# Earlier value-block loads, earlier first-pair steps, a split of the input scales, and FFN weight sums on VectorE in a hybrid attention, convolution and FFN block

## The chip, the cores and the metric

One NeuronCore of a Trainium2 chip runs the whole block. TensorE (PE) multiplies, with its weight loads shown as PEld; VectorE (DVE), ScalarE (ACT) and GpSimd (POOL) do the elementwise work; SyncE (SP) issues most of the DMAs, in the order of its own queue. The metric is device time in microseconds, the median of several runs. A profile is one execution with its trace.

## The reference

A decoder block over 1024 tokens of width 1024, everything in float32:

```python
h = rms_norm(x, g_pre_mix)
z = h @ w_in                     # q, k, v (3 groups x 8 heads x 64), conv input 2 x 1024, two gates 1024
y_attn = dilated_attention_mixer(q, k, v, rel_bias_table, w_attn_out)
y_conv = conformer_conv_mixer(glu_in, b_glu, w_dw, b_dw, g_ln, b_ln, w_conv_out, b_conv_out)
x = x + rms_norm((sigmoid(z_ga) * y_attn + sigmoid(z_gc) * y_conv) @ w_mix_out, g_post_mix)
h = rms_norm(x, g_pre_ffn)
gate, up = split(h @ w_ffn_in)   # 2 x 2816
x = x + rms_norm((silu(gate) * up) @ w_ffn_out, g_post_ffn)
```

The attention has three groups of eight heads (windows of 128, 512 and 2048 tokens with dilations 1, 4 and 16); the convolution is causal, depthwise, 31 wide, with a sigmoid gate before it and a layer norm and silu behind it.

## The kernel before

**Precision.** Each float32 operand is split into a high part and a low part of a short type, and a product is three matmuls (high by high, high by low, low by high). Weights are split into float16 parts with a scale that is a power of two, found from the weight itself: `peaks` (L122) squares the block on ACT (L129) with the row sums as a by-product, `total` rounds them (L135 or L137) and multiplies them with a matrix of ones on PE (L144), and `scales` turns the result into the scale on DVE (L145, L147, L155, L156). `scaled_parts` (L282) then makes the parts: ACT writes the high part (L283), DVE the low part (L284). The input's two scales, for the first half of the block (C_PRE) and for the FFN (C_PREF), are made the same way from the two gain vectors in `input_scales` (L165).

**Winograd pairs.** Most weights are handled as pairs of blocks, one Winograd step of 2 by 2 with seven products instead of eight (`winograd`, L455). Its products run into a few PSUM banks one after the other, X, Z and V: ACT copies X and V out at L464, L469 and L474, and the functions f11, f12, f21, f22 add the results on DVE. f22 (L1912 in the FFN, L987 for queries and keys) reads bank X, and the last product (A22 by T4) is added into X only after that. The sums of the weights' quarters are made in `quarters` (L296): step c = 1 makes two sums (L312, L313), c = 3 two more (L319, L320), and the steps c = 0, 2, 4, 5 split a block each. All four sums are issued on the engine `self.wsplit`, which is GpSimd while the convolution runs beside the pairs and again from L1697 on (that is, in the mixing product and the FFN). The right-hand side's sums are made in `quarter_sums` (L492): a first loop (L507, L508) and a second one (L516 on `wsplit`, L517 on DVE); each sum is split by ACT (L1339) and DVE (L1340).

**Order.** The order is written out by hand. Each engine runs its instructions in the order in which the program issues them, and the program issues matmuls and, between them, other steps. A `tick()` follows every third matmul of 512 columns (or every sixth of 256 columns in the value stage); `later(n, step)` puts a step n ticks after now, and generators given to `bg` are advanced by one step a tick. `ready(jobs, load, peaks, scales, parts)` (L374) plans the preparation of weight blocks: at which tick they are loaded, squared, scaled and split. `pair(i)` (L401) does this for the next Winograd pair while the present one is multiplied; `timed(now, then)` (L393) does it for the value blocks. `load_ahead(i)` issues the DMA loads (L259) of all blocks up to i that are not on their way yet, on SP's queue, each into a buffer: a slot "b" (42 of them), or, for the first block of a pair, one of three ring buffers "d". 

**Stages** (us in the profiled execution):

- *Start* (to 47): the first blocks against the raw input. `input_scales` is finished after the last matmul of the start; behind it stand the first gate's DVE additions (L735).
- *Gates, conv input* (to 160): single blocks, then the first two Winograd pairs. Their preparation is planned in `build` by one `ready` call and two `later` calls. In the same part of SP's queue stand the bias lines of the attention (L596) and their write to 1024 rows (L599).
- *Pairs of conv input, gates, queries and keys* (to 551), with the depthwise convolution on DVE, ACT and PE beside them.
- *Values* (551 to 710): six value blocks of 256 columns (`v`, L1069), matmuls L1090, L1092 and L1094 into two PSUM banks, evicted by ACT at L1100 and L1102 and stored at L1077. Beside them run the convolution's layer norm (`conv_norm`: statistics L531, DVE L1373 and L1379, ACT L1376, silu L1395, stores L1397) and the attention, which reads back queries and keys (L1015, L1016, L1022), the bias lines (L609) and values (L1052). L1188 are its first products.
- *Rest of the attention, output and mixing products* (to 1085).
- *FFN input* (1085 to 1493): PLAIN single blocks (L1796 silu, L1798 product), then twenty Winograd pairs (f11 L1907, f22 L1912, f12 L1916), and sums of the results for the output product (`sums`, L1773 to L1790), stored on SP; `plain_sums` does the latter for the single blocks.
- *FFN output* (to the end): L2021.

Of the kernel before, what the change touches and what calls it, by code (L numbers as in the profile page):

```python
# [20 lines left out]
KT = 8  # L21
# [44 lines left out]
def f(ap):  # L66
    return ap if ap.dtype == F16 else ap.bitcast(F32)


class Build:  # L70
# [94 lines left out]
    def input_scales(self):  # L165

        nc = self.nc
        self.gain, self.unscale, self.top = [], [], []
        p = []
        for c in (C_PRE, C_PREF):  # L170
            m = self.tiny(2, "pk", 4)
            nc.scalar.activation(self.junk[:, :8], self.col8(c), AF.Square, scale=1 / H_TOP, accum_out=m[:, 0:1])
            p.append(self.total(m, 1))
        yield 6
        for e, c in enumerate((C_PRE, C_PREF)):
            t = self.small.tile([128, 5], F32, name=f"hs{e}")
            self.bound(t[:, 0:1], p[e])
            nc.vector.reciprocal(t[:, 1:2], t[:, 0:1])
            for k, x in enumerate((1.0, -1.0, 0.125)):
                nc.vector.tensor_scalar(t[:, 2 + k:3 + k], t[:, 0:1], x, None, op0=OP.mult)  # L180
            g = self.small.tile([128, 8], F32, name=f"hg{e}")
            nc.vector.tensor_scalar(g, self.col8(c), t[:, 1:2], None, op0=OP.mult)
            self.gain.append(g)
            self.unscale.append(t[:, 2:5])
            self.top.append(t[:, 1:2])
            yield 1

    stag = "s"

# [200 lines left out]
        for k, x in zip(parts, todo, strict=True):  # L390
            self.later(k, x)

    def timed(self, now, then):  # L393

        self.load_ahead(now[-1])
        self.queue_split(now[-1])
        self.flush(now[-1])
        self.ready(then, 1, 8, 20, (22, 24, 27, 30)[:2 * len(then)])
        return [self.hl.pop(i) for i in now]

    def pair(self, i):  # L401


        J = self.jobs
        self.load_ahead(i)
        self.queue_split(i)
        self.flush(i)
        n, t = i + 1, self.ticks
        todo = [(1, lambda: self.quarters(i, 3)), (8, lambda: self.quarters(i, 4)), (10, lambda: self.quarters(i, 5))]
        if n < len(J) and J[n][2] == "row1":  # L410
            if n + 2 < len(J) and J[n + 2][2] == "row1":
                todo += [(LF, lambda: self.load_ahead(n + 3)), (PK, lambda: self.peaks(n + 3))]
            if n + 1 in self.pre:
                todo += [(PRE + c, lambda c=c: self.prescale(n + 1, c)) for c in range(2)]
            todo += [(SC, lambda: self.scales(n + 1))]
            todo += [(k, lambda c=c: self.quarters(n + 1, c)) for c, k in enumerate(PC)]
            if self.conv_sums:
                todo.append((22, self.channel_sum))
            self.queued = n + 2
        elif n < len(J):  # L420
            self.ready((n, n + 1), 2, 9, 18, (20, 22, 24, 26))
        for k, s in todo:
            self.plan.setdefault(t + k, []).append(s)
        return self.hl[i]
# [189 lines left out]
    def start(self, jobs):  # L614


        nc = self.nc
        n = len(jobs)
# [64 lines left out]
        for kt in range(KT):  # L683
            s = slice(kt * 128, (kt + 1) * 128)
            for i in range(n):
                for a, b in ((W[i][0], self.hH), (W[i][0], self.hL), (W[i][1], self.hH)):
                    for hf in range(2):
                        nc.tensor.matmul(banks[i][hf], a[:, s], b[kt][:, hf * H:(hf + 1) * H],  # L688
                                         start=kt == 0 and a is W[i][0] and b is self.hH,
                                         stop=kt == KT - 1 and a is W[i][1])  # L690
                self.tick()
            if kt == KT - 1:
                for _ in ns:
                    pass
            if kt == KT - 3:
                next(norm)
            if kt == KT - 2:
                try:
                    next(norm)
                except StopIteration as e:  # L700
                    pb = e.value
        self.rs = self.slot()
        for hf in range(2):
            nc.scalar.copy(self.rs[:, hf * H:(hf + 1) * H], pb[hf])
        self.xs = xs
        return banks

    def renorm(self):
# [357 lines left out]
        self.nc.gpsimd.tensor_tensor(d[:, :, 1], y, f(d[:, :, 0]), op=OP.subtract)  # L1066
        return v

    def v(self, g, hg, now, then):  # L1069

        nc = self.nc
        W = self.timed(now, then)
        un = self.scale[now[0]][1]

        def out(i, x):
# [416 lines left out]
def build(ctx, tc, aps):  # L1492
# [81 lines left out]
    conv = B.conv()  # L1574
    next(conv)
    i = glu_pairs[0]
    B.ready((i - 1, i), 10, 22, 30, (32, 33, 36, 38, 42))
    B.later(34, lambda: B.load_ahead(i + 2))
    B.later(44, lambda: B.peaks(i + 2))
    for j in range(3, FIRST):  # L1580
        u_out(j, B.glu(j, glu_jobs[j][1], B.gate(j, glu_jobs[j][0])))

# [51 lines left out]
    att = B.attention()  # L1634
    vs = list(vj.values()) + [late[:1] or co[:1]]
    for i, (g, hg) in enumerate(vj):
        B.v(g, hg, vs[i], vs[i + 1])
        if i == 0:
            next(att)
            B.fine = att  # L1640
# [152 lines left out]
    def ffn_half(j, hf, W):  # L1793
# [4 lines left out]
        nc.vector.scalar_tensor_tensor(o, ps, B.scale[fi[j][1]][1], o, op0=OP.mult, op1=OP.mult)  # L1798
        held[j, hf] = o

    Ws, i = [], fi[PLAIN][1]
    B.ready((i - 1, i), 1, 16, 28, (42, 44, 50))
    B.later(46, lambda: B.load_ahead(i + 2))
    B.later(58, lambda: B.peaks(i + 2))
    for j in range(PLAIN):
# [13 lines left out]
    for j in range(0, PLAIN, 2):  # L1819
# [8 lines left out]
                q.clear()  # L1828

        for n in range(3):  # L1830
            B.later(6 + 5 * n + j, lambda n=n, f=plain_sums: f(n))


    NP = FT // 2
# [302 lines left out]
```

## Time and profile before

| | |
|---|---|
| time, median of 3 runs | 1709.87 us (1708.0 to 1711.88) |
| the profiled execution | 1711.49 us |
| its span, mean granted clock | 1709.6 us, 0.991 |
| PE busy | 1654.3 us (97%), 8757 matmuls |
| DVE busy | 1272.2 us (74%) |
| ACT busy | 992.7 us (58%) |
| POOL busy | 599.0 us (35%), 468 instructions |

A row of the timeline gives the start, the length, the engine, the line, what it writes and reads, the shape, how many instructions of one kind the row holds, and in brackets the idle time in front of it with what ended it. SPq is a DMA in SP's queue, from the issue of the first to that of the last in the row. Windows give the same by stretches: busy time and count of each engine, the granted TensorE clock (1.00 is full), the share of the DMA engines and the bandwidth. A busy PE is not PE at its peak: at a clock of 0.50 it is busy as well.

### The profile page before, as it was taken

The page shows a single profiled execution, that of the slowest core. Times are in us where ns is not written, and L with a number is a line of the kernel's source. Part 1 is how long each engine was busy: PE and PEld are TensorE (multiplying, and loading weights), DVE is VectorE, ACT ScalarE, POOL GpSimd, SP SyncE. Part 2 cuts the span into 40 slices and gives each one's busy share as a digit, 9 for nine tenths or more (in the row PEclk, how much of TensorE's full clock was granted, in tenths as well). Part 3 has the DMA queues.
Part 4 walks back from the last instruction along what each step waited for, and adds up shares of the span by engine and source line. Part 5 has one row for each costly group of instructions (what it writes and reads, how often), then busy time and mean ns, then how long its engine had stood idle before and what let it go on. Part 6 is the DMA issues. An engine that isn't in the chain of part 4 may idle for free.

```text
span 1709.6 us, 25078 instructions
## 1 busy us (share of the span) xinstructions
PE 1654.3 (97%) x8757; PEld 1064.7 (62%) x8757; DVE 1272.2 (74%) x2383; ACT 992.7 (58%) x1875; POOL 599.0 (35%) x468
## 2 busy tenths in 40 slices
PE   8989999999999899989999999989999999999998
PEld 7634444444444789989888878534444444488886
DVE  6879999999999566698764756586666665677686
ACT  6475667766665587768622357654545545454463
POOL 0005777787785145646400120133342333100000
PEclk9999999999999999999999999999999999999999
DMA  4352334355656879887934732223233232394244
GB/s 166 114 188 97 105 140 150 135 186 180 202 161 170 255 237 252 220 229 217 314 142 184 276 127 87 80 76 116 93 123 118 92 130 93 128 376 136 98 137 154
DMA packets 159481, 277.06 MB, mean 162 GB/s; under 512 B 46993, under 2 KB 78412, under 8 KB 159356
## 3 DMA queue, kind: packets, MB, share of 16 engines
q1 hardware_dynamic: 155148, 263.30, 46.6%
q0 software_dynamic: 3920, 11.91, 2.2%
q8 instruction: 69, 1.13, 0.3%
q14 instruction: 56, 0.46, 0.1%
q10 hardware_dynamic: 288, 0.27, 0.0%
HBM read 184.81 MB, written 95.33 MB: 164 GB/s over the span
## 4 chain that ended last, share of the span: by engine, by line
PE 75%; DVE 10%; DMA 4%; ACT 4%; POOL 3%; issue 3%; SPq 1%; DVEq 0%; ACTq 0%; POOLq 0%
PE p L2021 12%; PE p L450 11%; PE p L452 11%; PE p L451 11%; PE p L1747 4%; PE p L434 4%; PE p L438 4%; PE p L436 4%; DVE p L829 3%; PE p L688 2%; PE p L1188 2%; PE p L1090 2%; PE p L1092 2%; PE p L1094 2%; PE p L1224 2%
## 5 line engine op out<-in xcount | busy, mean ns | idle before, releaser
L450 PE MATMUL p<-b,b 128*128 128x512 f16 x1032 | 393.1, 381 | 5.6 <-ACT c L464 5.0
L452 PE MATMUL p<-b,b 128*128 128x512 f16 x1032 | 393.3, 381 | 2.8 <-POOL b L293 2.8
L451 PE MATMUL p<-b,b 128*128 128x512 f16 x1032 | 393.2, 381 | 0.0
L2021 PE MATMUL p<-b,b 128*128 128x512 f32 x924 | 209.8, 390 | 0.0
L2021 PEld LDWEIGHTS p<-b,b 128*128 128x128 f32 x924 | 173.5, 188 | 36.1
L452 PEld LDWEIGHTS <-b 128*128 128x128 f16 x1032 | 101.0, 98 | 128.6 <-POOL b L293 6.5
L450 PEld LDWEIGHTS <-b 128*128 128x128 f16 x1032 | 101.2, 98 | 126.4 <-issue 6.3
L451 PEld LDWEIGHTS <-b 128*128 128x128 f16 x1032 | 101.0, 98 | 124.2 <-issue 8.5
L312 POOL TENSOR_TENSOR d<-b 128x512 f32<-128x512 f32 x42 | 60.5, 1440 | 306.0 <-DVE b L284 217.3
L829 DVE SCALAR_TENSOR_TENSOR p<-b,par,p 128x511 f32<-128x511 f32 (+14 forms) x232 | 163.9, 739 | 0.0
L434 PE MATMUL p<-b,b 128*128 128x512 f32 (+1 forms) x368 | 146.1, 397 | 4.7 <-ACT b L283 2.4
L438 PE MATMUL p<-b,b 128*128 128x512 f32 (+1 forms) x368 | 145.2, 394 | 0.1
L436 PE MATMUL p<-b,b 128*128 128x512 f32 (+1 forms) x368 | 145.1, 394 | 0.0
L293 POOL TENSOR_TENSOR b<-d,b 128x1024 f16<-128x1024 f32 x44 | 96.1, 2184 | 81.7 <-ACT b L292 81.5
L1090 PE MATMUL p<-b,b 128*128 128x256 f16 x384 | 107.1, 279 | 9.9 <-ACT d L1100 9.9
L284 DVE SCALAR_TENSOR_TENSOR b<-d,sc,b 128x1024 f16<-128x1024 f32 x40 | 53.1, 1328 | 75.1 <-ACT b L283 75.1
L1092 PE MATMUL p<-b,b 128*128 128x256 f16 x384 | 107.2, 279 | 0.0
L1094 PE MATMUL p<-b,b 128*128 128x256 f16 x384 | 107.1, 279 | 0.0
L1340 DVE TENSOR_TENSOR b<-b,b 128x512 fp32r<-128x512 f32 (+1 forms) x117 | 85.3, 731 | 22.7 <-ACT b L1339 21.3
L1339 ACT CAST b<-b 128x512 fp32r<-128x512 f32 (+1 forms) x117 | 72.0, 618 | 43.0 <-PE p L2021 18.0
L1340 DVE TENSOR_TENSOR b<-c,b 128x512 fp32r<-128x512 f32 (+1 forms) x101 | 70.3, 696 | 33.5 <-ACT b L1339 33.3
L1201 ACT ACTIVATE c<-c,stat 128x128 f32<-128x128 f32 (+1 forms) x192 | 84.8, 445 | 12.2 <-DVE stat L1191 12.0
(273 smaller groups left out, 3697.3 us busy)
## 6 DMA issues: line engine op xcount, KB each, us to landing
b<-w_in SPq DMA_DIRECT2D x30, 512.0 KB, 7.4
dk<-c SPq DMA_DIRECT2D x48, 256.0 KB, 2.6
dq<-c SPq DMA_DIRECT2D x48, 256.0 KB, 3.4
b<-dq SPq DMA_DIRECT2D x48, 256.0 KB, 8.7
b<-dk SPq DMA_DIRECT2D x48, 256.0 KB, 9.9
b<-w_fi SPq DMA_DIRECT2D x24, 512.0 KB, 4.9
d<-w_in SPq DMA_DIRECT2D x23, 512.0 KB, 4.8
dqS<-c SPq DMA_DIRECT2D x44, 256.0 KB, 2.0
```

The lines of the kernel that those rows point to most:

```text
L434: nc.tensor.matmul(ps, hi[:, s], a, start=kt == 0, stop=False)
L436: nc.tensor.matmul(ps, hi[:, s], b, start=False, stop=False)
L438: nc.tensor.matmul(ps, lo[:, s], a, start=False, stop=kt == nk - 1)
L450: nc.tensor.matmul(ps, hi[:, s], a, start=first and kt == 0, stop=False, skip_group_check=True)
L451: nc.tensor.matmul(ps, hi[:, s], b, start=False, stop=False, skip_group_check=True)
L452: nc.tensor.matmul(ps, lo[:, s], a, start=False, stop=kt == 3, skip_group_check=True)
L829: nc.vector.scalar_tensor_tensor(A[i][:, j:], src[i][:, :H - j], w[i], A[i][:, j:], op0=OP.mult, op1=OP.add)
L1090: nc.tensor.matmul(o, a, hi[:, s], start=kt == 0, stop=False)
L1092: nc.tensor.matmul(o, a, lo[:, s], start=False, stop=False)
L1094: nc.tensor.matmul(o, b, hi[:, s], start=False, stop=kt == KT - 1)
L1340: nc.vector.tensor_tensor(s[:, 512:512 + n], src, f(s[:, :n]), op=OP.subtract)
L2021: nc.tensor.matmul(acc[t], x, y, start=first and e == 0, stop=last and e == 2, skip_group_check=True)
```

## The change

Five edits, all in the order of steps or the engine of one operation; the arithmetic is the same.

1. `input_scales` yields between its two sets. `start` calls for the first one a step of kt earlier (KT-2), and the second one runs as a background generator after the start.
2. `timed` no longer loads the next value block at tick 1. It loads two blocks ahead at tick 14, and the steps for the next block are at 17 and 19 to 25 where they were at 20 and 22 to 30. The last pair of queries and keys loads the second value block at its tick 16.
3. The first Winograd pairs: load at tick 2 (was 10), squares at 14 (22), scale at 24 (30), parts from 26 (32); the second pair's load at 22 (34) and squares at 37 (44).
4. `wsplit` is set to VectorE before the FFN. So 84 GpSimd additions of 128x512 (L312, L313, L319, L320 of twenty pairs, and four of L516) go to DVE.
5. The FFN's first pair: squares at tick 12 (16), scale at 22 (28), parts at 24, 26, 30 (42, 44, 50); `plain_sums` 24 ticks later.

```diff
--- before.py
+++ after.py
@@ -173,6 +173,8 @@
             p.append(self.total(m, 1))
         yield 6
         for e, c in enumerate((C_PRE, C_PREF)):
+            if e:
+                yield 12
             t = self.small.tile([128, 5], F32, name=f"hs{e}")
             self.bound(t[:, 0:1], p[e])
             nc.vector.reciprocal(t[:, 1:2], t[:, 0:1])
@@ -183,7 +185,6 @@
             self.gain.append(g)
             self.unscale.append(t[:, 2:5])
             self.top.append(t[:, 1:2])
-            yield 1
 
     stag = "s"
 
@@ -390,12 +391,14 @@
         for k, x in zip(parts, todo, strict=True):
             self.later(k, x)
 
-    def timed(self, now, then):
+    def timed(self, now, then, after):
 
         self.load_ahead(now[-1])
         self.queue_split(now[-1])
         self.flush(now[-1])
-        self.ready(then, 1, 8, 20, (22, 24, 27, 30)[:2 * len(then)])
+        self.ready(then, None, 8, 17, (19, 21, 23, 25)[:2 * len(then)])
+        if after:
+            self.later(14, lambda: self.load_ahead(after[-1]))
         return [self.hl.pop(i) for i in now]
 
     def pair(self, i):
@@ -419,6 +422,7 @@
             self.queued = n + 2
         elif n < len(J):
             self.ready((n, n + 1), 2, 9, 18, (20, 22, 24, 26))
+            self.later(16, lambda: self.load_ahead(n + 3))
         for k, s in todo:
             self.plan.setdefault(t + k, []).append(s)
         return self.hl[i]
@@ -689,11 +693,10 @@
                                          start=kt == 0 and a is W[i][0] and b is self.hH,
                                          stop=kt == KT - 1 and a is W[i][1])
                 self.tick()
-            if kt == KT - 1:
-                for _ in ns:
-                    pass
             if kt == KT - 3:
                 next(norm)
+            if kt == KT - 2:
+                next(ns)
             if kt == KT - 2:
                 try:
                     next(norm)
@@ -703,6 +706,7 @@
         for hf in range(2):
             nc.scalar.copy(self.rs[:, hf * H:(hf + 1) * H], pb[hf])
         self.xs = xs
+        self.bg(ns)
         return banks
 
     def renorm(self):
@@ -1066,10 +1070,10 @@
         self.nc.gpsimd.tensor_tensor(d[:, :, 1], y, f(d[:, :, 0]), op=OP.subtract)
         return v
 
-    def v(self, g, hg, now, then):
-
-        nc = self.nc
-        W = self.timed(now, then)
+    def v(self, g, hg, now, then, after):
+
+        nc = self.nc
+        W = self.timed(now, then, after)
         un = self.scale[now[0]][1]
 
         def out(i, x):
@@ -1574,9 +1578,9 @@
     conv = B.conv()
     next(conv)
     i = glu_pairs[0]
-    B.ready((i - 1, i), 10, 22, 30, (32, 33, 36, 38, 42))
-    B.later(34, lambda: B.load_ahead(i + 2))
-    B.later(44, lambda: B.peaks(i + 2))
+    B.ready((i - 1, i), 2, 14, 24, (26, 27, 31, 34, 40))
+    B.later(22, lambda: B.load_ahead(i + 2))
+    B.later(37, lambda: B.peaks(i + 2))
     for j in range(3, FIRST):
         u_out(j, B.glu(j, glu_jobs[j][1], B.gate(j, glu_jobs[j][0])))
 
@@ -1634,7 +1638,7 @@
     att = B.attention()
     vs = list(vj.values()) + [late[:1] or co[:1]]
     for i, (g, hg) in enumerate(vj):
-        B.v(g, hg, vs[i], vs[i + 1])
+        B.v(g, hg, vs[i], vs[i + 1], vs[i + 2] if i < 5 else None)
         if i == 0:
             next(att)
             B.fine = att
@@ -1798,8 +1802,9 @@
         nc.vector.scalar_tensor_tensor(o, ps, B.scale[fi[j][1]][1], o, op0=OP.mult, op1=OP.mult)
         held[j, hf] = o
 
+    B.wsplit = nc.vector
     Ws, i = [], fi[PLAIN][1]
-    B.ready((i - 1, i), 1, 16, 28, (42, 44, 50))
+    B.ready((i - 1, i), 1, 12, 22, (24, 26, 30))
     B.later(46, lambda: B.load_ahead(i + 2))
     B.later(58, lambda: B.peaks(i + 2))
     for j in range(PLAIN):
@@ -1828,7 +1833,7 @@
                 q.clear()
 
         for n in range(3):
-            B.later(6 + 5 * n + j, lambda n=n, f=plain_sums: f(n))
+            B.later(30 + 5 * n + j, lambda n=n, f=plain_sums: f(n))
 
 
     NP = FT // 2
```

In the changed program the lines stand up to five further down: L259 is L260, L312 and L313 are L313 and L314, L964 is L968, L1912 is L1917.

SP's queue around the first read-back of queries and keys (w_v are the value weights, two DMAs a block, here the third block; dconv the convolution's blocks, dq and dk queries and keys, rep the bias lines). Before:

```order
L1356 DMA b_5201<-dconv_70 128x1024
L1356 DMA b_5230<-dconv_71 128x1024
L1356 DMA b_5263<-dconv_72 128x1024
L1015 DMA b_5381<-dq_98 64x1024
L1016 DMA b_5382<-dq_98 64x1024
L1015 DMA b_5385<-dq_98 64x1024
L1016 DMA b_5386<-dq_98 64x1024
L1022 DMA b_5389<-dk_97 64x1024 x2
L1022 DMA b_5392<-dk_97 64x1024 x2
L609 DMA c_5395<-rep_699 128x2x256
L259 DMA b_5404<-w_v 128x1024
L259 DMA b_5406<-w_v 128x1024
```

After:

```order
L1360 DMA b_5201<-dconv_70 128x1024
L260 DMA b_5224<-w_v 128x1024
L260 DMA b_5226<-w_v 128x1024
L1360 DMA b_5234<-dconv_71 128x1024
L1360 DMA b_5277<-dconv_72 128x1024
L1019 DMA b_5385<-dq_98 64x1024
L1020 DMA b_5386<-dq_98 64x1024
L1019 DMA b_5389<-dq_98 64x1024
```

The third value block's load has moved from behind the read-backs to between two loads of the convolution. The second block's, further up in the same queue, has moved ahead of four stores of queries and keys and one store of the convolution; the fourth block's from behind the first two silu stores (L1397) to right behind the next value read-back (L1052), and the fifth's to behind the silu stores, ahead of the next read-back of queries and keys.

DVE in one of the twenty FFN pairs, from the second split of the pair's late quarters to f12 (c_13073 to c_13075 are the pair's result halves, p the banks, d_13165 the next pair's two sums). Before:

```order
L1907 TENSOR_TENSOR c_13073<-p_13072,c_13073 128x512
L284 SCALAR_TENSOR_TENSOR c_13121<-b_12860,sc_12942,c_13121 128x512
L284 SCALAR_TENSOR_TENSOR b_13156<-d_12996,sc_13085,b_13156 128x1024
L1912 TENSOR_TENSOR c_13075<-p_13071,c_13075 128x512
L1916 TENSOR_TENSOR c_13074<-p_13131,c_13074 128x512
L284 SCALAR_TENSOR_TENSOR b_13193<-d_13165,sc_13085,b_13193 128x1024
```

After:

```order
L1912 TENSOR_TENSOR c_13073<-p_13072,c_13073 128x512
L285 SCALAR_TENSOR_TENSOR c_13121<-b_12860,sc_12942,c_13121 128x512
L285 SCALAR_TENSOR_TENSOR b_13156<-d_12996,sc_13085,b_13156 128x1024
L313 TENSOR_TENSOR d_13165<-b_12998 128x512
L314 TENSOR_TENSOR d_13165<-d_13165,d_12996 128x512
L1917 TENSOR_TENSOR c_13075<-p_13071,c_13075 128x512
L1921 TENSOR_TENSOR c_13074<-p_13131,c_13074 128x512
L285 SCALAR_TENSOR_TENSOR b_13193<-d_13165,sc_13085,b_13193 128x1024
```

The two sums stand between the split of the next pair's first block and f22; before, they were on POOL.

ACT at the first Winograd pair (b_787 and b_883 are single blocks, d_ and b_ behind L129 the pair's two weight blocks, pb their rounded row sums). Before:

```order
L283 ACTIVATE b_957<-b_787,sc_935 128x512
L1339 CAST b_966<-b_249 128x512
L737 ACTIVATE b_885<-p_931,par,sc_820 128x512
L129 ACTIVATE junk,pk_990<-b_883 128x1024
L137 CAST pb_992<-pk_990 128x1
L1339 CAST b_1000<-c_997 128x512
L1339 CAST b_1000<-b_250 128x512
L129 ACTIVATE junk,pk_1016<-d_947 128x1024
L129 ACTIVATE junk,pk_1016<-b_949 128x1024
L135 ACTIVATE pb_1019<-pk_1016 128x1
```

After:

```order
L129 ACTIVATE junk,pk_972<-d_899 128x1024
L129 ACTIVATE junk,pk_972<-b_901 128x1024
L135 ACTIVATE pb_975<-pk_972 128x1
L284 ACTIVATE b_957<-b_787,sc_939 128x512
L1343 CAST b_966<-b_249 128x512
L741 ACTIVATE b_885<-p_935,par,sc_820 128x512
L129 ACTIVATE junk,pk_995<-b_883 128x1024
L137 CAST pb_997<-pk_995 128x1
L1343 CAST b_1005<-c_1002 128x512
L1343 CAST b_1005<-b_250 128x512
```

The pair's squares have moved from behind the single block's square to seven places further up.

## The prediction

> **What bounds the kernel now.** I read the page's busy shares and the chain that ended last, then what the matmul engine (PE) waited for, then windows around each wait, then the timeline there.
>
> ```profile
> span 1709.6 us, 25078 instructions
> PE 75%; DVE 10%; DMA 4%; ACT 4%; POOL 3%; issue 3%; SPq 1%; DVEq 0%; ACTq 0%; POOLq 0%
> ```
>
> The last chain runs three quarters of the span through PE, so time is won only where PE stands still or runs at a reduced clock. The list of PE's waits (total, times, longest) says where:
>
> ```profile
> PE p L1090 <- ACT d L1100: 9.9, 2, 6.3
> PE p L450 <- ACT c L464: 5.0, 1, 5.0
> PE p L144 <- ACT pb L135: 4.5, 3, 2.7
> PE p L450 <- DVE c L987: 3.1, 4, 1.2
> PE p L434 <- ACT b L283: 2.4, 1, 2.4
> PE p L434 <- DVE b L735: 2.3, 1, 2.3
> PE p L1473 <- ACT b L1479: 1.9, 2, 1.1
> ```
>
> All but the L987 line belong to places that the change touches: the start (2.3), the first two Winograd pairs (2.4 and, of L144's three, 0.45 and 2.7), the value stage (9.9), the front of the FFN (5.0, L144's third of 1.4, and 0.8 of L1473's). The granted clock adds to them. Windows (length, then busy time and count of PE, its weight loads, DVE, ACT, POOL, then clock, DMA share, GB/s):
>
> ```profile
> 47.50:50.00 2.50, 2.50 (x12) 2.05 (x11) 2.29 (x4) 0.52 (x1) 0.00 (x0) 1.00 0.00 0
> 107.50:110.00 2.50, 2.50 (x7) 0.83 (x8) 2.43 (x8) 1.17 (x3) 0.00 (x0) 0.50 0.00 0
> 125.00:127.50 2.50, 2.50 (x7) 0.89 (x6) 0.00 (x0) 2.50 (x4) 0.00 (x0) 0.50 0.88 320
> 590.00:595.00 5.00, 3.96 (x20) 2.83 (x19) 0.00 (x0) 2.82 (x5) 1.49 (x2) 0.50 0.33 96
> 595.00:600.00 5.00, 5.00 (x49) 4.64 (x48) 2.63 (x5) 1.29 (x3) 2.28 (x2) 0.99 0.04 12
> 620.00:625.00 5.00, 4.70 (x23) 3.96 (x23) 1.25 (x8) 4.97 (x8) 1.49 (x2) 0.50 0.86 326
> 1130.00:1135.00 5.00, 2.05 (x5) 0.69 (x5) 4.93 (x12) 3.50 (x7) 0.00 (x0) 0.60 0.01 2
> 1135.00:1140.00 5.00, 5.00 (x18) 2.01 (x17) 4.93 (x8) 1.80 (x3) 0.00 (x0) 0.71 0.31 116
> ```
>
> After most of these stalls the clock is 0.50: 7 matmuls of 512 columns in 2.5 us instead of 12, so such a window loses about 1.1. In the value stage 20 matmuls took 3.96 where 49 take 5.00, a loss of 1.9; after its second stall 23 took 4.70, a loss of 2.3. The FFN's two windows lose 0.97 and 1.1. A stall therefore costs its length and 1 to 2 us more.
>
> **The change, part by part.** Sums are made against the profiled execution: 1711.49 us, which is the span and 1.9 around it. The median of the runs is 1709.87, 1.6 lower.
>
> *Input scale.* Before, DVE works out two sets behind the start's last matmul:
>
> ```profile
> 44.45 0.16 DVE L145 TENSOR_SCALAR hs<-p 128x1 int32<-128x1 int32 x1 [7.81 <-PE p L144]
> 45.97 1.28 DVE L735 TENSOR_TENSOR b<-p,b 128x512 f32<-128x512 f32 x2
> ```
>
> L735 makes the gate that the next matmul waits for. Both sets stand in front of it (44.45 to 45.97). Now the first is done a step of the start earlier, inside the 7.81 in which DVE was idle, and the second comes a few ticks later on an idle DVE. L735 needs only its bank and the norm, both there before the last matmul. The 2.3 goes: **2.25**, with no loss of clock to win (47.5 to 50 stands at 1.00).
>
> *First pairs.* The loads of the first pair pass the 1024-row write of the bias line in SP's queue, those of the second pass a line write, a store and the next such write; squares, scale and parts move up with them.
>
> ```profile
> 99.94 1.06 ACT L129 ACTIVATE junk<-d 128x1024 bf16<-128x1024 f32 x1 [2.42 <-DMA d<-w_in]
> 102.75 0.16 PE L144 MATMUL p<-pb,ones 128*128 128x1 bf16 x1 [0.45 <-ACT pb L135]
> 123.02 0.16 PE L144 MATMUL p<-pb,ones 128*128 128x1 bf16 x1 [2.71 <-ACT pb L135]
> ```
>
> ACT waited 2.42 for the weights, and everything behind was late: 0.45 here, the 2.4 of L434 next, 1.1 of clock; at the second pair 2.71 and 1.1. Together 7.8. What is late next: the pair's two squares (1.06 each, some 2.4 with what belongs to them) now stand ahead of the early block's square on ACT, and PE comes to the two blocks' L144s one behind the other. If ACT's former idle time of 2.42 takes them in, nothing is lost; if they simply push the early block's square back, PE stands up to 2.4. I take 1.8, nearer to the upper end, since that idle time now lies behind the squares and only casts stand between. **6.0** is left (5 to 7.8).
>
> *Value stage.* Before, a value block is loaded when the one ahead of it starts:
>
> ```profile
> 563.44 3.02 SPq L1356 DMA_DIRECT2D b<-dconv  x4
> 577.52 1.41 SPq L259 DMA_DIRECT2D b<-w_v  x2
> 587.57 1.06 ACT L129 ACTIVATE junk<-b 128x1024 bf16<-128x1024 f32 x1 [7.67 <-DMA b<-w_v]
> 609.25 1.29 SPq L259 DMA_DIRECT2D b<-w_v  x2
> 617.02 1.06 ACT L129 ACTIVATE junk<-b 128x1024 bf16<-128x1024 f32 x1 [1.36 <-DMA b<-w_v]
> 625.79 3.44 SPq L1022 DMA_DIRECT2D b<-dk  x4
> ```
>
> The third block's load is issued at 577.52, behind the stacked queries and keys, and lands 10 us later. ACT stands 7.67 in front of its square, and the eviction L1100, queued behind the square, frees PE's bank 6.3 too late. Now that load stands among the convolution's loads of 563.44, 11 to 14 us earlier, so it lands by about 576 and the square does not wait. 6.3 and 1.9 of clock go: 8.2. At 609.25 the same happens with the fourth block (stall 9.9 - 6.3 = 3.6, clock 2.3); its load now stands right behind the value load of 584.80, ahead of eight stores. 14.1 in all. The loads need free slots: if one waits, the key stores and convolution loads queued behind it on SP wait too.
>
> What is late next here: ACT's waits of 1.47 and 1.36 go, which brings the second eviction 2.8 of the 3.6 forward, so up to 0.8 stays; the first exponentials follow ACT's chain, about 1.1; the second stack's key loads (625.79) are needed some 4 earlier by PE, stand behind one more megabyte of value weights, and are issued only about 2 earlier. Nothing to 2.7 for that; I take 1.6. **10.6** (8 to 13).
>
> *FFN front.* Blocks, sums of the right-hand side and the first pair meet here:
>
> ```profile
> 1127.38 1.75 DVE L517 SCALAR_TENSOR_TENSOR b<-b,b 128x512 f32<-128x512 f32 x1
> 1131.80 0.62 ACT L1339 CAST b<-b 128x512 f16<-128x512 f32 x1 [1.50 <-DVE b L517]
> 1133.45 0.68 DVE L517 SCALAR_TENSOR_TENSOR b<-b,b 128x512 f32<-128x512 f32 x1
> 1134.06 0.68 DVE L1778 TENSOR_TENSOR c<-c,c 128x512 f32<-128x512 f32 x1
> ```
>
> L517 takes 0.68 alone and 1.75 while POOL adds. ACT's copy L464, for which PE waits 5.0, stands behind casts that wait for these sums. From 1102 to 1131 I count 9.4 of such excess on DVE. The added work there is POOL's 12 adds, on DVE 0.61 to 0.68 each, 7.5; the plain sums (4 of 0.68, 2.7) go 24 ticks out, with their stores, whose readers come after the FFN. So DVE has 4.6 less to do; and the pair's scale and first parts move from ticks 28 and 42 to 22 and 24, into time in which DVE waited for ACT. By that count the copy is in time. At stake: 0.84 + 1.38 + 4.95 + 2.07 of clock = 9.2; I leave 0.4 for something new. **8.8** (6 to 9.2).
>
> *The twenty FFN pairs.* 80 of the 84 moved adds. PE waits for nothing there now, so nothing can be won; but the two adds L312 and L313 now stand on DVE right ahead of L1912, which must empty a bank before PE's last product.
>
> ```profile
> 1118.69 0.68 DVE L507 TENSOR_TENSOR c<-b,b 128x512 f32<-128x512 f32 x1
> 1119.40 0.69 DVE L508 SCALAR_TENSOR_TENSOR b<-c,b 128x512 f32<-128x512 f32 x1
> 1323.95 1.28 DVE L284 SCALAR_TENSOR_TENSOR b<-d,sc,b 128x1024 f16<-128x1024 f32 x1 [3.46 <-ACT b L283]
> 1325.15 0.68 DVE L1912 TENSOR_TENSOR c<-p,c 128x512 f32<-128x512 f32 x1
> 1327.26 0.38 PE L450 MATMUL p<-b,c 128*128 128x512 f16 x1
> 433.13 1.06 DVE L987 TENSOR_TENSOR c<-p,c 128x512 f32<-128x512 f32 x1
> 434.24 0.38 PE L450 MATMUL p<-b,c 128*128 128x512 f16 x1 [1.21 <-DVE c L987]
> L313 POOL TENSOR_TENSOR d<-d,d 128x512 f32<-128x512 f32 x18 | 28.4, 1578 | 1.4
> ```
>
> A dependent step takes 0.71 (L507 to L508), an independent one 0.61 (L517 to L1778). So L1912 starts at 1325.15 + 0.71 + 0.61 = 1326.47 and ends at 1327.15; PE follows a DVE end by 0.05 (434.19 to 434.24): 1327.20, where it needs 1327.26. It fits by 0.06, and I cost it at **0**. The cover is only that: each 0.1 us more is 2 us over 20 pairs.
>
> Sum: 2.25 + 6.0 + 10.6 + 8.8 = 27.65; 1711.49 - 27.65 = 1683.8, from the median 1682.2. I say **1683**.
>
> **A rule on the clock.** The rows: a stall of 2.3 left the clock at 1.00, stalls of 2.4 and 2.7 were followed by 0.50. [...]
>
> **Rivals.** *New waits keep part of it.* Each estimated residual doubles (3.5 in the value stage, 1.8 at the first pairs) and two of them are followed by a half-clock window (1.1 to 2.3): 5 to 8 back, about 1690. For: the loads of keys and the squares merely change places. Against: ACT has idle time at each place.
>
> *The early loads wait for slots.* Then SP moves nothing forward in the value stage and its 10.6 is lost: 1694. Against: SP idles after 577 and the raw blocks of the Winograd pairs have been released by then.
>
> *L1912 a little late.* If an add takes 0.1 to 0.3 longer, PE waits 0.2 to 0.5 in each pair: 4 to 10 us, about 1690. For: the margin of 0.06; the same kind of wait stands in the list as L987, four times, up to 1.2.
>
> *Slower.* The same place, if the adds keep the price they have now, 1.58 on POOL (DVE's L517 had 1.75 beside it): 3.16 instead of 1.32 puts L1912 1.84 later, 1.78 beyond the margin, times 20 pairs is 36: 1719. It turns the sign from 1.4 per pair (27.65 / 20). Against: with POOL empty DVE's rows are 0.68.
>
> **How the numbers follow.** Forecast 1683: 0.53. New waits: 0.18, loads without effect: 0.08, L1912 a little late: 0.11; slower: 0.05; several of these together, ending near the old time: 0.05. A measurement of this kernel tells about 0.2% (3.4 us) from no change; the first four cases are faster by more: 0.90, same 0.05, slower 0.05. The parts' low ends (2.2, 5, 8, 6) with 8 us for L1912 give 1697; their high ends give 1678. Range 1676 to 1699.
>
> **What would show it.** Right: no L735, L464 or L283 line among PE's waits, L1100's below 2; squares of value weights without a wait for DMA; no window below 0.9 at 107, 125, 590, 1132; L507 and L517 near 0.69 from 1102 on; L1912's successor without a wait in the pairs. Wrong: a PE wait for L1912's DVE result twenty times over, a wait for the key loads above 3 near 635, SP standing at a value load.

## The result, and the profile after

The changed kernel takes **1684.97 us** (median of 4 runs, 1684.47 to 1685.31), the kernel before 1710.88 beside it; the ratio is 0.9845, interval 0.9821 to 0.9869. The prediction was 1683, in a range of 1676 to 1699. The span of the profiled execution fell from 1709.6 to 1682.6. Lines are those of the changed kernel from here on, four or five higher than before, unless a kernel is named; each experiment's lines are its own.

What PE waited for in the changed kernel:

```profile
PE p L692 <- ACT b L666: 6.4, 1, 6.4
PE p L1192 <- DMA b<-dk: 4.1, 3, 2.4
PE p L454 <- DVE c L991: 3.1, 4, 1.2
PE p L1251 <- DVE c L1234: 2.9, 6, 1.4
...
PE p L454 <- ACT c L468: 1.6, 1, 1.6
PE p L438 <- ACT b L284: 1.5, 2, 0.9
...
PE p L454 <- DVE c L1917: 0.5, 1, 0.5
```

The waits for the value blocks' evictions (9.9), for the second gate's DVE work at the start (2.3) and for the rounded row sums pb of weight blocks (4.5) are gone. The FFN's wait for the copy of bank X, L468, is 1.6 where it was 5.0. The first row is the wait for the first loads at the start (6.1 before). Behind it a wait for keys has come up, 4.1 where it was 1.4. The wait for L991 belongs to a place that the change doesn't touch; it stayed at 3.1. L1251's operands are waited for 2.9, where it was 5.5 (L1247 before).

Both kernels issue the same 8757 matmuls, so the start of the n-th, counted from the start of the first, can be compared. What the changed kernel is ahead (us), at places in and between the stages:

| up to | matmul | ahead | gained there | forecast |
|---|---|---|---|---|
| middle of the start | 150 | 1.0 | 1.0 | 0 |
| behind the start | 300 | 3.7 | 2.6 | 2.25 |
| behind the first pairs | 600 | 10.8 | 7.1 | 6.0 |
| first value block | 2600 | 10.7 | -0.1 | 0 |
| third value block | 2960 | 25.2 | 14.5 | 14.1 |
| second stack's scores | 3110 | 16.6 | -8.5 | -3.5 |
| attention, up to 788 us | 4600 | 19.6 | 2.9 | 0 |
| before the FFN | 5900 | 19.6 | 0.0 | 0 |
| FFN front | 6300 | 27.3 | 7.7 | 8.8 |
| the twenty pairs, to the end | 8750 | 27.3 | 0.0 | 0 |

The 1.0 in the first row is the spread of the first loads: the same kernel, profiled once more, was ahead by 0.0 there. In that second profile the stages gain 2.6, 7.1, 14.6, -8.9, 2.9 and 7.7, so they repeat within 0.4; what differs is 3.5 us lost between matmuls 4600 and 4900, of which more below.

Where the value stage gives back is seen in four views of the changed kernel: SP's queue and ACT's squares in the timeline, PE's waits in it, and windows (length, busy time and count of PE, PEld, DVE, ACT, POOL, then clock, DMA share, GB/s):

```profile
551.84 0.87 SPq L260 DMA_DIRECT2D b<-w_v  x2
588.21 12.55 SPq L1401 DMA_DIRECT2D dact<-b  x8
600.85 1.28 SPq L260 DMA_DIRECT2D b<-w_v  x2
602.22 0.45 SPq L1019 DMA_DIRECT2D b<-dq  x1
606.10 4.55 SPq L1026 DMA_DIRECT2D b<-dk  x4
```

```profile
569.44 1.04 ACT L129 ACTIVATE junk<-b 128x1024 bf16<-128x1024 f32 x1
```

```profile
616.33 0.42 PE L1192 MATMUL p<-b,b 128*128 128x128 f32 x2 [1.16 <-DMA b<-dk]
619.15 0.66 PE L1192 MATMUL p<-b,b 128*128 128x128 f32 x2 [2.40 <-DMA b<-dk]
```

```profile
585.00:590.00 5.00, 5.00 (x48) 4.47 (x46) 4.45 (x4) 4.97 (x7) 0.00 (x0) 1.00 0.20 81
600.00:605.00 5.00, 4.16 (x34) 3.29 (x32) 2.49 (x16) 4.97 (x15) 1.49 (x2) 1.00 0.95 327
...
617.50:620.00 2.50, 0.84 (x4) 0.81 (x5) 0.15 (x1) 0.00 (x0) 1.17 (x2) 0.50 1.18 263
620.00:622.50 2.50, 2.50 (x15) 2.25 (x14) 1.03 (x5) 1.29 (x5) 0.00 (x0) 0.50 1.07 197
622.50:625.00 2.50, 2.50 (x17) 2.37 (x16) 0.77 (x3) 0.07 (x1) 0.00 (x0) 0.66 1.03 239
```

The third value block is issued at 551.84 and squared at 569.44 without a wait; the stall of 6.3 has no successor there. But the second stack's queries and keys stand in SP's queue behind eight silu stores of half a megabyte, whose issue follows ACT's silus (588.21 to 600.76), and behind the fifth value block. They are issued from 602 on, when the DMA engines are full (0.95 and more), while at 585 to 590 these stood at 0.20. PE reaches the second stack's last scores at 615, waits 3.6 in two pieces, and the clock stands at 0.50 behind them: 15 matmuls in 2.5 us where 24 or 25 are usual in this stage.

### The profile page after: what moved, and what is told of

Its sections match the earlier page's. It is cut to its first block, busy times and chain, and to the rows that moved or that the text cites. A ratio compares the mean times of both kernels' runs of the same rounds, so it can differ in the third digit from the quotient of the medians.

```text
span 1682.6 us, 25027 instructions
## 1 busy us (share of the span) xinstructions
PE 1644.7 (98%) x8757; PEld 1060.7 (63%) x8757; DVE 1275.8 (76%) x2467; ACT 995.4 (59%) x1875; POOL 468.0 (28%) x384
## 4 chain that ended last, share of the span: by engine, by line
PE 77%; DVE 9%; ACT 4%; POOL 3%; issue 3%; DMA 2%; DVEq 0%; SPq 0%; POOLq 0%; ACTq 0%
PE p L2026 12%; PE p L454 11%; PE p L456 11%; PE p L455 11%; PE p L1751 4%; PE p L438 4%; PE p L442 4%; PE p L440 4%; DVE p L833 3%; PE p L692 2%; PE p L1098 2%; PE p L1094 2%; PE p L1096 2%; PE p L1192 2%; PE p L1228 1%
## 5 line engine op out<-in xcount | busy, mean ns | idle before, releaser
L2026 PE MATMUL p<-b,b 128*128 128x512 f32 x924 | 209.8, 389 | 0.0
L438 PE MATMUL p<-b,b 128*128 128x512 f32 (+1 forms) x368 | 144.8, 393 | 1.5 <-ACT b L284 1.5
L442 PE MATMUL p<-b,b 128*128 128x512 f32 (+1 forms) x368 | 143.9, 391 | 0.4 <-DVE b L285 0.4
L1094 PE MATMUL p<-b,b 128*128 128x256 f16 x384 | 105.9, 276 | 0.1
L1096 PE MATMUL p<-b,b 128*128 128x256 f16 x384 | 106.0, 276 | 0.0
L1098 PE MATMUL p<-b,b 128*128 128x256 f16 x384 | 105.9, 276 | 0.0
L1344 DVE TENSOR_TENSOR b<-b,b 128x512 fp32r<-128x512 f32 (+1 forms) x117 | 80.1, 688 | 19.7 <-ACT b L1343 18.2
L1751 PE MATMUL p<-b,b 128*128 128x512 f32 x384 | 90.1, 392 | 0.0
```

The source lines that it names most:

```text
L438: nc.tensor.matmul(ps, hi[:, s], a, start=kt == 0, stop=False)
L442: nc.tensor.matmul(ps, lo[:, s], a, start=False, stop=kt == nk - 1)
L1094: nc.tensor.matmul(o, a, hi[:, s], start=kt == 0, stop=False)
L1096: nc.tensor.matmul(o, a, lo[:, s], start=False, stop=False)
L1344: nc.vector.tensor_tensor(s[:, 512:512 + n], src, f(s[:, :n]), op=OP.subtract)
L1751: nc.tensor.matmul(banks[tt][nh], st, wt[:, nh * H:(nh + 1) * H], start=bool(kt == 0 and a), stop=bool(kt == KT - 1 and b))
```

## The experiments

### Parts alone

Four kernels make parts of the change to the kernel before, so lines are those of before here (in the value kernel up to three higher).

The FFN's additions alone:

```diff
+    B.wsplit = nc.vector
     Ws, i = [], fi[PLAIN][1]
```

> The kernel before with wsplit set to VectorE before the FFN and nothing else. Contention theory (GpSimd's and VectorE's additions slow each other, and that made L464 late): L517 and L1340 near 0.69 us between 1102 and 1131, PE's wait for L464 falls from 5.0 to below 1.5, the two half-clock windows at 1130 to 1140 go, L144's 1.4 and L1473's 0.8 there stay: 6 to 7 us less than before, ratio 0.996. Plan theory (the late ticks of the pair's scale and parts made it late): at least 3.5 of the 5.0 stays, 0 to 2 us less. In the pairs both expect no wait for f22 (L1912) beyond one.

Measured: ratio 0.9978 (0.9958 to 0.9998). PE's wait for the copy and one DVE row beside it:

```profile
PE p L450 <- ACT c L464: 3.3, 1, 3.3
```

```profile
1120.53 0.68 DVE L517 SCALAR_TENSOR_TENSOR b<-b,b 128x512 f32<-128x512 f32 x1
```

The FFN's plan alone:

```diff
-    B.ready((i - 1, i), 1, 16, 28, (42, 44, 50))
+    B.ready((i - 1, i), 1, 12, 22, (24, 26, 30))
...
-            B.later(6 + 5 * n + j, lambda n=n, f=plain_sums: f(n))
+            B.later(30 + 5 * n + j, lambda n=n, f=plain_sums: f(n))
```

> The kernel before with the FFN's first pair and plain sums at the new ticks, additions still on GpSimd. Contention theory: the wait for L464 stays at 3 or more, L517 stays above 1.5 us beside GpSimd; only L144's 1.4 and L1473's 0.8 may go: 0 to 3 us less. Plan theory: the wait for L464 goes as in the changed kernel (to 1.6) and its half-clock windows with it: 7 us less.

Measured: ratio 0.9987 (0.9969 to 1.0005). The same two views:

```profile
PE p L450 <- ACT c L464: 5.0, 1, 5.0
```

```profile
1120.60 1.76 DVE L517 SCALAR_TENSOR_TENSOR b<-b,b 128x512 f32<-128x512 f32 x1
```

Neither theory is right by itself. With the additions moved, DVE's sums take 0.68, yet 3.3 of the wait stays; what this kernel lacks there against the changed one is the plan (1.6 with it). With the plan moved, 5.0 stays; what this one lacks is the move of the additions, and L517 still takes 1.76. From matmul 5900 to 6300 the additions alone gain 3.9, the plan alone 3.0, both 7.7: a little more than their sum. The plan alone takes away L1473's wait of 0.8, at matmul 6015.

The value blocks alone:

```diff
-        self.ready(then, 1, 8, 20, (22, 24, 27, 30)[:2 * len(then)])
+        self.ready(then, None, 8, 17, (19, 21, 23, 25)[:2 * len(then)])
+        if after:
+            self.later(14, lambda: self.load_ahead(after[-1]))
```

(with the second block's load at tick 16 of the last query and key pair)

> The kernel before with the value blocks' new loads and ticks and nothing else. Theory that the stages add up: both waits for L1100 go (14 us with the clock's loss), some 8 to 9 come back as waits for the second stack's keys and a half-clock stretch, 3 return in the attention: 8 to 10 us less, 1701 to 1703. Rival (what is won here is only pushed into the DVE-bound attention behind it): less than 4 us.

Measured: 1701.26 us, ratio 0.9933 (0.9908 to 0.9958). Ahead by 14.5 at matmul 2960, 6.7 at 3110, 9.4 at 4600, 9.9 before the FFN: the same course as in the whole change. By the ratio it is 11.5 us less (7.2 to 15.8), where 8 to 10 were expected.

The first pairs alone:

```diff
-    B.ready((i - 1, i), 10, 22, 30, (32, 33, 36, 38, 42))
-    B.later(34, lambda: B.load_ahead(i + 2))
-    B.later(44, lambda: B.peaks(i + 2))
+    B.ready((i - 1, i), 2, 14, 24, (26, 27, 31, 34, 40))
+    B.later(22, lambda: B.load_ahead(i + 2))
+    B.later(37, lambda: B.peaks(i + 2))
```

> The kernel before with the first Winograd pairs' new ticks and nothing else (not the input's scales). Theory that the stages add up: 7 us less, as the changed kernel shows at that place; waits for L434 1.5 in all, none for L144 above 0.5. Rival (the conv input's pairs behind it, which wait for other things, take it back): less than 3 us.

Measured: ratio 0.998 (0.9964 to 0.9995), 0.9 to 6.2 us. The profile is 7.3 ahead at matmul 600, of which 7.1 were gained at the first pairs, and still 7.4 at 4600. At 4900 it is 3.4: four are lost in the attention near 815 us, in waits for loads that the change doesn't touch (2.5 and 1.3) and in a half-clock stretch twice as long as before's, which lasted 3.41. The changed kernel profiled again (below) lost 3.5 at that place against its own first profile. So this is a place where executions differ. But ten runs together also show less than 7.1, and whether what is missing belongs to this edit stays open. The input scale's split was not run alone; this kernel is without it and gains 0.0 between matmuls 150 and 300, where every kernel with it gains 2.6.

### The margin of f22

In the changed kernel a steady FFN pair runs like this, on DVE and then on PE:

```profile
1151.77 1.28 DVE L285 SCALAR_TENSOR_TENSOR b<-d,sc,b 128x1024 f16<-128x1024 f32 x1 [3.19 <-ACT b L284]
1152.97 0.68 DVE L313 TENSOR_TENSOR d<-b 128x512 f32<-128x512 f32 x1
1153.69 0.69 DVE L314 TENSOR_TENSOR d<-d,d 128x512 f32<-128x512 f32 x1
1154.30 0.68 DVE L1917 TENSOR_TENSOR c<-p,c 128x512 f32<-128x512 f32 x1
```

```profile
1155.08 0.38 PE L454 MATMUL p<-b,c 128*128 128x512 f16 x1
```

f22 (L1917) ends at 1154.98, PE follows a DVE end by 0.05 (434.19 to 434.24 in the kernel before), and the product starts at 1155.08 without a wait: 0.05 to spare, where the forecast had 0.06. Making one of the two sums twice should show it:

```diff
-            add(self.s12[:, l], a21, a22, op=OP.add)
+            for _ in range(2 if self.ffn else 1):
+                add(self.s12[:, l], a21, a22, op=OP.add)
```

> The changed kernel with the first of the two sums in front of f22 made twice in the twenty FFN pairs (the same result written again), so f22 comes 0.6 to 0.7 us later. Margin theory (f22 had 0.05 to 0.06 us to spare): PE waits some 0.6 for L1917's result in each pair, 11 to 13 us slower than the changed kernel, 1696 to 1698. Rival (f22 has slack that the rows don't show, the price of the move is nothing whatever stands there): below 3 us slower.

Measured: 1700.94 us, ratio 0.9914 (0.9896 to 0.9933), which is 0.0069 or 11.8 us above the changed kernel's 0.9845 (each ratio is measured against the kernel before on the same chip). PE's waits in the FFN input, then a pair on DVE and PE:

```profile
PE p L456 <- DVE c L1920: 10.5, 19, 1.2
```

```profile
1159.24 1.41 DVE L315 TENSOR_TENSOR d<-b 128x512 f32<-128x512 f32 x2
1160.68 0.69 DVE L316 TENSOR_TENSOR d<-d,d 128x512 f32<-128x512 f32 x1
1161.29 0.68 DVE L1920 TENSOR_TENSOR c<-p,c 128x512 f32<-128x512 f32 x1
```

```profile
1162.03 0.38 PE L456 MATMUL p<-b,c 128*128 128x512 f16 x1 [0.52 <-DVE c L1920]
```

One more step of 0.7 on DVE became a wait in 19 pairs. In the matmul count the loss grows by 0.68 per pair, 11.6 from matmul 6300 to the end. The cover of the move is as thin as computed, and one step of 0.69 beyond it costs all of its length.

The other way round, the two sums one tick earlier, in DVE's idle time ahead of the split:

```diff
-            todo += [(k, lambda c=c: self.quarters(n + 1, c)) for c, k in enumerate(PC)]
+            todo += [(k, lambda c=c: self.quarters(n + 1, c)) for c, k in enumerate((18, 17, 26) if self.ffn else PC)]
```

> The changed kernel with the two sums one tick ahead of the next pair's first split, so they fill VectorE's idle time and f22 follows the split at once. Margin theory: f22 ends 1.2 to 1.4 us earlier, PE had no wait there, so nothing is won: within 2 us of the changed kernel's 1685. Rival (small delays of f22 were taking time all along): 2 to 8 us faster.

Measured: 1686.64 us, ratio 0.9833 (0.9814 to 0.9851), and no change from matmul 6300 to the end (0.0). f22 then follows the split at once (split at 1150.92, f22 at 1152.12), and nothing is won in the steady pairs, as there was no wait. Only the first pair, in the FFN's front, had one, the 0.5 for L1917 in the list above; it goes, and the front gains 0.6.

### What is late next in the value stage

The fifth value block behind the second stack's loads:

```diff
-            self.later(14, lambda: self.load_ahead(after[-1]))
+            self.later(self.va, lambda: self.load_ahead(after[-1]))
...
+        B.va = 20 if i == 2 else 14
```

> The changed kernel with the fifth value block's load at tick 20 of the third block, behind the loads of the second stack of queries and keys. Theory (that load's megabyte stands ahead of the keys, 1.3 us of issue and some 2.7 of transfer): PE's waits for dk at 615 to 620 (3.6 in all) fall below 1 and the half-clock windows at 617 to 625 go, 4 to 6 us there, of which up to 3.5 may come back at 730: 1 to 5 us faster than the changed kernel, 1680 to 1684. Rival (the DMA engines are full from 590 to 625 and the order doesn't matter): within 1.5 us.

Measured: 1681.21 us, ratio 0.9805 (0.9787 to 0.9823). Between 600 and 640 PE waits for no key, all windows there stand at a clock of 1.00, and the kernel is 5.6 ahead of the changed one at matmul 3110. From matmul 2960 to 3110 alone it gains 6.3. At the end it is still 5.3 ahead: little comes back.

The second stack's queries and keys ahead of the silu stores (a call in `conv_norm` in front of its last loop):

```diff
+        pre = [self.stacks(*order[0])]
+        self.early = lambda: [self.stack_load(pre[0], i) for i in range(4)]
...
         pb = yield from self.rstd(q[0], T, self.eps_ln, 8)
+        self.early()
```

> The changed kernel with the second stack's queries and keys read ahead of the eight silu stores, when the DMA engines stand at 0.2 to 0.9 (575 to 590). Theory (the keys are late because they stand behind 5 MB in the queue): no PE wait for dk above 0.5 between 600 and 640 and no window below 0.9 there, 6 to 8 us earlier at 635, of which 3 to 4 come back by 745 as the attention's own VectorE chain is next: 3 to 5 us faster than the changed kernel. Rival (attention bound by its own chain): all comes back, within 1.5 us.

Measured: 1679.69 us, ratio 0.9794 (0.9778 to 0.9809). SP's queue, and a window where the changed kernel stood still:

```profile
576.50 0.45 SPq L1019 DMA_DIRECT2D b<-dq  x1
...
579.00 3.22 SPq L1026 DMA_DIRECT2D b<-dk  x4
588.88 12.56 SPq L1406 DMA_DIRECT2D dact<-b  x8
```

```profile
615.00:620.00 5.00, 5.00 (x50) 4.82 (x49) 3.95 (x13) 3.22 (x12) 0.90 (x1) 1.00 1.04 243
```

The loads go into and just ahead of the stretch in which the DMA engines stood at 0.33 and 0.20 in the changed kernel (580 to 590). PE has no wait for keys between 600 and 640, and 5.2 are ahead at matmul 3110 (6.3 of them gained from 2960 on), 5.6 at the end. Both kernels contradict the rivals: the order does matter while the DMA engines are full (0.95 and more from 600 to 625 in the changed kernel), and the attention doesn't take it back. They contradict my expectation too that three or more come back there. The kernel before this one moves only one megabyte behind the keys; that was enough.

### What is left of the FFN front

In the changed kernel DVE waits 2.9 for a cast that stands behind ACT's squares of the second pair, and the moved additions L320, L321 stand ahead of the third of the last sums:

```profile
1099.65 1.29 DVE L1344 TENSOR_TENSOR b<-b,b 128x512 f16<-128x512 f32 x2 [2.86 <-ACT b L1343]
...
1104.11 0.68 DVE L320 TENSOR_TENSOR b<-d,b 128x512 f32<-128x512 f32 x1
```

The squares earlier, alone and together with the second stack's early loads, beside the changed kernel again:

```diff
-    B.later(46, lambda: B.load_ahead(i + 2))
-    B.later(58, lambda: B.peaks(i + 2))
+    B.later(30, lambda: B.load_ahead(i + 2))
+    B.later(46, lambda: B.peaks(i + 2))
```

> The changed kernel with the FFN's second pair loaded at tick 30 and squared at tick 46. If ScalarE's squares hold up the casts: PE's wait for L468 below 0.3 and 1.3 to 1.6 us less; if VectorE's own work is the limit: the wait stays above 1.

> The second stack's queries and keys read ahead of the silu stores, and, at the FFN's front, the second pair's load at tick 30 and its squares at tick 46 (46 and 58), so that ScalarE's casts of the right-hand side's last sums no longer stand behind the squares (VectorE waits 2.9 for those casts at 1097 to 1100 in the changed kernel). If VectorE's chain through those casts sets L468, PE's last wait there, 1.6, goes below 0.3; with the value stage's 5 to 6 us: 6.5 to 7.5 us less span than the changed kernel, some 0.996 of its time. Rival (L468 is late by VectorE's own work, whenever the squares come): the wait stays above 1, 5 to 6 us less.

> The changed kernel again, beside the two below on one chip: 0.98 to 0.99 of the kernel before.

Measured: the changed kernel again 1685.86 us, ratio 0.9848 (0.9828 to 0.9868); with both edits 1679.72, ratio 0.9811 (0.9789 to 0.9832); the squares alone 1682.88 in one run. In both kernels with earlier squares the wait for L468 went from 1.6 to 1.1, and DVE's gap only moved (2.4 in front of a cast at 1092.70 in the kernel with the squares alone). So the rival holds for 1.1 of the 1.6. From matmul 6060 to 6300 both gain 0.4 on the changed kernel, where 1.3 to 1.6 were hoped for. The last kernel takes two of the moved additions out of the way (with the second stack's early loads):

```diff
-        todo = [(1, lambda: self.quarters(i, 3)), ...
+        todo = [(5 if self.ffn else 1, lambda: self.quarters(i, 3)), ...
```

> The second stack's queries and keys read ahead of the silu stores, and in the FFN's pairs the second two quarter sums (L320, L321) at the pair's tick 5 in place of 1. In the changed kernel they stand on VectorE ahead of the third of the last right-hand sums, 1.2 us, for whose casts ScalarE and then L468 wait. If the added sums themselves make what is left of that wait, PE's wait for L468 goes from 1.6 to about 0.4, and the span is 6.5 to 7.5 us below the changed kernel's; in the later pairs no new wait. If not: the wait stays above 1.

Measured: 1680.35 us, ratio 0.9801 (0.978 to 0.9822). PE's waits in its FFN input:

```profile
PE p L455 <- DVE c L1924: 1.1, 1, 1.1
PE p L455 <- ACT c L474: 0.4, 1, 0.4
PE p L455 <- ACT c L469: 0.3, 1, 0.3
```

The wait for the copy falls to 0.3 as expected, but 1.5 come up at two later places of the same pair, and the front gains 0.0 on the changed kernel. None of the three orders (this one, the earlier squares, the two sums a tick earlier) has less than 1.6 of waits at the front. That DVE's work itself would have to shrink is a guess from this; it wasn't tried.

## Why the prediction was right

**Input scale.** Forecast 2.25, gained 2.6. The waiting DVE row is gone from PE's list, and the second set runs behind the gates' first additions on an idle DVE.

**First pairs.** Forecast 6.0, gained 7.1. The new wait that I priced at 1.8 is there in another shape: L438 for ACT's L284, 1.5 in two pieces, and 0.4 for L442, none of them at L144; and no window from 100 to 130 is below a clock of 1.00, as hoped. The excess is clock: I counted 1.1 for each half-clock window of 2.5, but each of the two stretches lasted 3.41 (107.03 to 110.44, 124.09 to 127.51) and cost 1.7.

**Value stage.** The 14.1 that the stalls and the clock cost came as 14.5. The residual was mis-sized: 3.5 forecast, 8.5 measured at matmul 3110. The step is the term for the second stack's loads, "Nothing to 2.7 for that; I take 1.6". The two kernels that get these keys in time gain 6.3 on the changed one from 2960 to 3110 and still give back 2.3, close to the 0.8 and 1.1 of my other two terms. So the keys cost 6.3: waits of 3.6, the rest mainly the half-clock stretch behind them. I had named the megabyte of value weights ahead of the keys; my price left out that it and the silu stores fill the DMA engines just then (0.95 at 600 to 605, 1.18 at 617.5 to 620), and that the clock stood at 0.50 behind this wait, until 624.18. My own first rival named this: the residual more than doubled. The sign that I gave for being wrong, a wait for the key loads above 3 near 635 (617 in the changed kernel), did appear, as 3.6 in two pieces.

The forecast for the stage still held, 8.9 in all against 10.6, because 2.9 was gained again in the attention, which I had not counted. These are PE's waits for L1230 (now L1234) between 640 and 800, first before, then after:

```profile
PE p L1247 <- DVE c L1230: 3.8, 4, 1.7
```

```profile
PE p L1251 <- DVE c L1234: 1.0, 3, 0.4
```

My list of waits had left that row out. The gain of 2.7 to 2.9 is in every profile of a kernel with the value edit (the one with the value blocks alone too), and 0.4 at most in the three kernels without it, so it belongs to the edit; why DVE's chain is earlier there I did not follow.

**FFN front.** Forecast 8.8, gained 7.7. The mechanism was right and needed both edits (3.9 and 3.0 alone). "By that count the copy is in time" was 1.6 too good: I had 0.4 for something new, and my sign of being right, no line for L464 or L283 (now L468 and L284), was not met.

**The twenty pairs.** Forecast 0 with 0.06 to spare; measured 0.0 with 0.05, and the slope beyond the margin, 0.68 a pair for a step of 0.69, is that of the slower rival. By that slope (an estimate, not run) the change would have lost if the additions had kept the price that they have beside a working POOL.

**The sum.** The parts were off by 0.4, 1.1, -1.7 and -1.1 and nearly cancel: 27.65 forecast, 26.3 gained without the 1.0 of the first loads. That 1683 came so near to 1684.97 is in part luck, above all the 2.9.

**The clock.** Stalls of 1.6 (FFN front, after) and 2.3 (start, before) left it at 1.00; 2.4 and 2.7 (before) and 3.6 in two pieces (after) were followed by 0.50. With the first pairs' new ticks the changed kernel has no half-clock window there: its clock is 1.00 from 9.8 to 617.3. But the length alone doesn't decide. In the kernel with the FFN's additions alone, whose first pairs are those of before, the second stall cost no clock:

```profile
122.79 0.16 PE L144 MATMUL p<-pb,ones 128*128 128x1 bf16 x1 [2.50 <-ACT pb L135]
```

```profile
125.00:127.50 2.50, 2.50 (x13) 1.14 (x12) 0.00 (x0) 2.50 (x3) 0.00 (x0) 1.00 0.89 345
```

And of two stalls of 1.7 in the attention of the kernel before, in front of L1247 at 740.96 and at 825.56, the first left the clock at 1.00 and the second was followed by 0.50, from 827.24 on. So the loss of clock at the second pair is not certain, and up to 1.7 of the 7.1 hangs on it. In the clock records of the kernel before and of the changed one every half-clock stretch, the one at the very end apart, lasts 3.41 us (at 107.03, 124.09 and 827.24 before) or 6.83 us (at 588.31, 619.03 and 1131.03 before, at 617.35 after).

The fastest kernels are those with the second stack read early: 1679.69 us, ratio 0.9794 to the kernel before, about 0.5% below the change itself (0.9845 and 0.9848). With one more edit each they are the same within their intervals (0.9811 and 0.9801).

## What to carry to other kernels

When a stall is removed, the next thing late is often what shared the queue with it: look at who is issued behind the moved transfer, and whether the DMA engines are already full when it comes; an idle stretch shortly before is where to put it. When work moves to another engine, find the instruction there that a tensor product waits for and compute its margin in hundredths of a microsecond, since one more step per pair was 11.8 us here. A shortage on one engine can come out at another place when its work is only put in another order, as it did at the FFN front when two additions were made later.

## What the runs showed of the hardware

In the FFN's pairs DVE lost time beside POOL in an instruction with both operands in SBUF, and none in one with an operand in PSUM. Groups by line over the FFN's pairs, before (POOL adding) and after (POOL empty); the columns are count, busy time, mean ns, and idle time before:

```profile
L1929 DVE SCALAR_TENSOR_TENSOR c<-p,sc,c 128x512 f32<-128x512 f32 x19 | 14.1, 744 | 0.4
L1783 DVE TENSOR_TENSOR c<-c,c 128x512 f32<-128x512 f32 x9 | 13.8, 1535 | 0.3
```

```profile
L1934 DVE SCALAR_TENSOR_TENSOR c<-p,sc,c 128x512 f32<-128x512 f32 x18 | 13.5, 748 | 0.4
L1787 DVE TENSOR_TENSOR c<-c,c 128x512 f32<-128x512 f32 x9 | 6.2, 693 | 0.3
```

L1929 with one operand in PSUM took 744 ns beside POOL and 748 without it (L1934); L1783 with both operands in SBUF took 1535 and then 693 (L1787).

The price is not a fixed factor. Two additions on DVE and the POOL addition that each met, before:

```profile
1166.65 1.64 DVE L1783 TENSOR_TENSOR c<-c,c 128x512 f32<-128x512 f32 x1
1185.60 0.85 DVE L1778 TENSOR_TENSOR c<-c,c 128x512 f32<-128x512 f32 x1
```

```profile
1166.09 1.65 POOL L312 TENSOR_TENSOR d<-b 128x512 f32<-128x512 f32 x1 [9.39 <-DVE b L284]
1184.24 1.66 POOL L312 TENSOR_TENSOR d<-b 128x512 f32<-128x512 f32 x1 [11.47 <-DVE b L284]
```

POOL ends at 1167.74 and 1185.90, DVE 0.55 later both times, although one DVE addition had started 1.09 and the other 0.30 ahead of that end. Their excess over 0.69, 0.95 and 0.16, is what was left of POOL's instruction, less 0.14. In the FFN input of the kernel before, all 33 additions of L1778, L1783, L1785 and L1790 that began inside a POOL addition end 0.55 behind it, and the 8 that met none took 0.69.
